# The last MLP of a three-block transformer kernel: the down projection turned, with tokens instead of features on the PSUM partitions

## The chip, the cores and the metric

The kernel runs on one core of one Trainium2 chip. The metric is the device time of one execution in microseconds (us); less is better. The runs of the kernel before gave a median of 1609.58 us.

## The reference, cut to what matters

A chain of three blocks works on 256 latent tokens of 1024 features (and 256 context tokens in the first two). The change lies in the last step of the third block alone: the squared-ReLU MLP with its residual, and the final norm.

```python
def rmsnorm(x, g):
    xf = x.astype(jnp.float32)
    y = xf * lax.rsqrt(jnp.mean(xf * xf, axis=-1, keepdims=True) + NORM_EPS)
    return (y * g.astype(jnp.float32)).astype(x.dtype)
...
D_FF_2 = 4 * D_MODEL          # 4096
...
# last step of the block: h = rmsnorm(x, norm_mlp_g); a = relu(h @ w_up) ** 2; x = x + a @ w_down
# result: rmsnorm(x, norm_final_g)
```

The last two lines are a summary in the kernel's terms. Everything is float32, and the kernel keeps that accuracy by splitting each operand into a high and a low part.

## The kernel before, in words

Activations lie with features on the 128 partitions: `x` is a tile of 8 feature tiles by 512 tokens, and `xs[k]` (128 features by 256 tokens) are the latent tokens' columns. Every float32 product is made of three fp32r products on TensorE, hi x hi, lo x hi and hi x lo (`mm3`, which calls `mm`, L365). A weight chunk is 128 partitions by 1024 numbers, 512 KB. It is loaded on SP's queue into one of 4 buffers `raw` (L349), then `split` makes its high part on ScalarE (`whi`, L343) and its low part on VectorE (`wlo`, L344). `whi` and `wlo` have 3 buffers each, so the split of a chunk waits until TensorE has let go of the chunk three before it. Engines take their instructions in the order that the program's scheduler wrote down; the order cannot change at run time.

The last MLP is the end of `second` (from L1562). Its steps:

- Four chunks `w_ocb` finish the cross attention's output projection (`out2`). Each adds two feature tiles to `x` (L1617).
- `prep` (L520, L521) makes the pair `hm` from `x` times the norm's gains. `sumcols` squares `x` (L552, ScalarE) and sums the squares over the features with a matmul against ones into the bank `ps_nr`; after a small matmul against a constant, `rsqrt` (L398 to L409, nine short VectorE steps) and `bcast` give the row `bcs` of every token's factor, which the first activation needs.
- Up: 32 chunks `w_u`, each one output tile of 128 features by 256 tokens, 8 x 3 = 24 matmuls with the weights stationary and 256 token columns streaming, into one of 4 banks `ps_mm`. The evacuation `ev` is a chain over three engines: VectorE `r` (L1579), GpSimd `a` (L1580), ScalarE `ach` (L343), VectorE `acl` (L344).
- Down: four groups of 8 chunks `w_d`. A chunk of group g holds the weights of one output tile for 8 of the 32 tiles of the activation: again 24 matmuls with stationary weights and 256 streaming columns, into one of two banks `ps_dn`. After each chunk VectorE adds the bank to `x` (L1549). In the last group ScalarE also makes `out`, `x` times the final gains (L1597).
- `AHEAD = 1`: before the down chunks of group g the up chunks run to one beyond the 8 that the group needs.
- Final norm (`rstd_bc`, run as soon as it can be): the squares of seven feature tiles are made between the last down chunks and summed over the features by matmuls against ones (L365, `ps_nr<-sq,ones`); the eighth tile's squares, the root, a broadcast over the partitions by TensorE and eight multiplications follow the last down product (L1601, L1603). Four DMAs of 256 KB write the result.

Of the kernel before, what the change touches and what calls it, by code (L numbers as in the profile page):

```python
# [10 lines left out]
F32 = mybir.dt.float32  # L11
# [8 lines left out]
P = 128  # L20
# [5 lines left out]
# phases in which a product's lo x hi pass comes before its hi x lo pass  # L26
SWAP = ()
# convolutions that take the token after before the token before
TAPS = ('bcw{}', 'fcw0_{}')
# phases that take (y * w) * y in the root's last step, not (y * y) * w  # L30
ROOT = ('pre', 'gmlp', 'gdn', 'ffn0', 'mla', 'ffn1', 'sparse')
MARK = lambda name: None
def weave(*gens):
    """runs the generators step by step in turn."""
    gens = list(gens)
    while gens:
        for g in list(gens):
            if next(g, 0) == 0:
                gens.remove(g)
# [20 lines left out]
# ---------------------------------------------------------------- host layout  # L60
def _fm(w, rows=None):
    """[K, n*128] -> [n, 128, (K/128)*128]: chunk n holds output tile n for every k tile."""
    k, n = w.shape
    return w.reshape(k // P, P, n // P, P).transpose(2, 1, 0, 3).reshape(n // P, P, k)


def _fmx(w, cols):
    """[K, cols] with cols <= 128 -> [1, 128, (K/128)*cols]."""
# [4 lines left out]
def _tm(w, kk):  # L73
    """[K, n*512] -> [n * K/(128*kk), 128, kk*512]."""
# [5 lines left out]
def _cols(v):  # L80
    """[n*128] -> [128, n]."""
# [14 lines left out]
def _consts():  # L96
# [15 lines left out]
    # rows of the (k_idx 64, k_rope 32, w_idx 8) tile spread over 128 partitions  # L112
# [10 lines left out]
    # rope tables, features on partitions  # L123
# [32 lines left out]
def _layout(x):  # L156
    """Lays the inputs out for the chip: name -> array."""
# [4 lines left out]
    x0 = np.concatenate([x["ctx"][0].T, x["x"][0].T], 1)  # [1024, 512]  # L162
# [25 lines left out]
    vec["nfin"] = _cols(x["norm_final_g_2"])  # L188
# [19 lines left out]
    # halves of the input features, two output tiles a chunk  # L208
# [20 lines left out]
    uk = x["w_uk_2"][0]  # [8, 64, 128]  # L229
# [5 lines left out]
    # halves of the input features, two output tiles a chunk  # L235
# [10 lines left out]
    o["w_d2"] = np.stack([_fm(dn[a * 1024:(a + 1) * 1024]) for a in range(4)], 0).reshape(32, P, 1024)  # L246
# [14 lines left out]
# ---------------------------------------------------------------- chip  # L261
class K:
# [25 lines left out]
    def psum(self, **tags):  # L288
        """opens the PSUM banks of a phase: tag -> banks; those of the phase before are closed."""
# [9 lines left out]
    def outer(self, **tags):  # L299
        """closes all PSUM pools; the banks given here outlive the phases that follow."""  # L300
# [18 lines left out]
    def nr(self):  # L319
        """the bank that the norms use."""  # L320
# [20 lines left out]
    # ---- basics  # L341
# [25 lines left out]
    def mm3(self, out, a, b, start, stop):  # L367
        """out += a^T b with a, b as (hi, lo) pairs."""
# [6 lines left out]
    def behind(self, *ins):  # L375
        """what is emitted inside takes its engines' turns after the instructions ins."""
# [13 lines left out]
    def rsqrt(self, v, n, scale=1.0, eps=EPS, plus=None):  # L390
        """(v * scale + eps) ** -0.5 for a [128, n] tile: a guess from the bits, a Newton and a cubic step.
        plus: a tile with eps * RSQ already in it that takes the place of eps."""
# [27 lines left out]
    def rstd_bc1(self, pool, tiles, T):  # L420
        """[128, T] with (mean of the squares over the features in tiles + eps) ** -0.5 of every token."""
# [27 lines left out]
        if n * (T // H) <= 4 and T > H:  # L449
            # groups of 32 rows: one per tile and half  # L450
# [23 lines left out]
    def rstd0(self, pool, tiles):  # L474
        """rstd_bc for 512 tokens, the squares on two engines."""
# [22 lines left out]
    def norm1(self, pool, tiles, T, A, B, hi, lo, halves, bc=None):  # L498
        """hi, lo = split(x * rstd * A + B), A and B per feature (and per half)."""
# [16 lines left out]
    def prep(self, tiles, g, hi, lo):  # L516
        """hi, lo = split(x * g), g per feature; the products' columns get the token's factor later."""
# [5 lines left out]
    def prepb(self, pool, tiles, A, B, hi, lo, soon=True):  # L523
        """hi, lo = split([x * A | B | B]): products with them, their columns times the row returned, plus column
        256, are those with the normalised x * A + B."""
# [16 lines left out]
    def sumcols(self, tiles, T, col=None, tag="nr", pool=None):  # L542
        """[128, T / 128] in PSUM: the sum over all features of (x * col)^2 of every token."""
# [1370 lines left out]
```

## Time and profile before

| what | value |
|---|---|
| median of the runs | 1609.58 us (1602.55, 1609.58, 1613.06) |
| profiled execution, span from first to last instruction | 1609.9 us |
| TensorE busy, share of the span | 97% |
| VectorE, ScalarE, GpSimd busy | 71%, 48%, 13% |
| moved by DMA | 246.27 MB, 153 GB/s |

For the profiled execution the trace gives the span only; no time around it is listed, and the span lies 0.3 us above the median of the runs. Busy time of TensorE counts every matmul from its start to its modelled end, and neighbours overlap, so a fully busy TensorE can still be made faster by issuing fewer columns or fewer matmuls. Starts are exact to 0.01 us, so the spacing of two starts is what a matmul costs.

### The profile page before, as it was taken

The page shows a single profiled execution, that of the slowest core. Times are in us where ns is not written, and L with a number is a line of the kernel's source. Part 1 is how long each engine was busy: PE and PEld are TensorE (multiplying, and loading weights), DVE is VectorE, ACT ScalarE, POOL GpSimd, SP SyncE. Part 2 cuts the span into 40 slices and gives each one's busy share as a digit, 9 for nine tenths or more (in the row PEclk, how much of TensorE's full clock was granted, in tenths as well). Part 3 has the DMA queues.
Part 4 walks back from the last instruction along what each step waited for, and adds up shares of the span by engine and source line. Part 5 has one row for each costly group of instructions (what it writes and reads, how often), then busy time and mean ns, then how long its engine had stood idle before and what let it go on. Part 6 is the DMA issues. An engine that isn't in the chain of part 4 may idle for free.

```text
span 1609.9 us, 28341 instructions
## 1 busy us (share of the span) xinstructions
PE 1553.9 (97%) x10912; PEld 1345.7 (84%) x10912; DVE 1149.8 (71%) x2440; ACT 780.4 (48%) x1422; POOL 202.7 (13%) x191
## 2 busy tenths in 40 slices
PE   7999889999999999999999999999999999999997
PEld 4767667888888888888877799998898898899996
DVE  4556863667999894875676688987897666666663
ACT  4377743445332332353554565656455555444443
POOL 0412100100120120100000021212332000011100
PEclk9999995999999999999999999999999999999999
DMA  8356531343557674633123456565444254345552
GB/s 342 115 201 186 166 105 55 101 139 128 171 183 219 217 234 141 204 118 131 50 63 97 130 173 187 171 193 193 153 127 152 66 176 152 105 157 184 184 183 67
DMA packets 97127, 246.27 MB, mean 153 GB/s; under 512 B 25312, under 2 KB 38368, under 8 KB 96480
## 3 DMA queue, kind: packets, MB, share of 16 engines
q1 hardware_dynamic: 96704, 243.93, 46.9%
q8 instruction: 86, 1.41, 0.4%
q10 hardware_dynamic: 288, 0.52, 0.1%
q14 instruction: 49, 0.40, 0.1%
HBM read 236.30 MB, written 8.13 MB: 152 GB/s over the span
## 4 chain that ended last, share of the span: by engine, by line
PE 88%; DVE 5%; DMA 3%; ACT 2%; issue 1%; SPq 0%; DVEq 0%; ACTq 0%
PE ps_mm L365 52%; PE ps_dn L365 17%; PE ps_nr L365 5%; PE ps_s L365 4%; PE ps_su L365 3%; PE ps_po L365 2%; PE ps_lv L365 1%; DVE wlo L344 1%; DMA rawa<-in_ada 1%; PE ps_ad L365 1%; PE ps_pt L388 1%; ACT whi L343 1%; DMA kvl<-kvd 1%; PE ps_kv L365 1%; PE ps_sm L365 1%
## 5 line engine op out<-in xcount | busy, mean ns | idle before, releaser
L343 ACT ACTIVATE whi<-raw 128x1024 fp32r<-128x1024 f32 (+2 forms) x345 | 346.5, 1008 | 417.5 <-PE ps_mm L365 203.5
L344 DVE TENSOR_TENSOR wlo<-raw,whi 128x1024 fp32r<-128x1024 f32 (+2 forms) x334 | 399.9, 1200 | 128.1 <-ACT whi L343 126.1
L365 PE MATMUL ps_mm<-fh,whi 128*128 128x258 f32 (+2 forms) x728 | 241.6, 333 | 2.6 <-ACT fh L512 1.6
L365 PE MATMUL ps_mm<-fh,wlo 128*128 128x258 f32 (+2 forms) x728 | 241.3, 332 | 0.0
L365 PE MATMUL ps_mm<-fl,whi 128*128 128x258 f32 (+2 forms) x728 | 241.2, 332 | 0.0
L365 PEld LDWEIGHTS ps_mm<-fh,whi 128*128 128x128 f32 x728 | 138.2, 190 | 15.8 <-ACT fh L512 1.8
L365 PEld LDWEIGHTS ps_mm<-fl,whi 128*128 128x128 f32 x728 | 138.3, 190 | 12.7
L365 PEld LDWEIGHTS ps_mm<-fh,wlo 128*128 128x128 f32 x728 | 137.9, 190 | 13.2 <-issue 0.4
L812 POOL TENSOR_TENSOR act<-cg,cu 128x512 f32<-128x512 f32 (+1 forms) x44 | 76.3, 1734 | 465.0 <-DVE cu L750 314.5
L365 PE MATMUL ps_dn<-ah,whi 128*128 128x256 f32 (+1 forms) x366 | 115.8, 319 | 1.6 <-ACT whi L343 1.2
L365 PE MATMUL ps_dn<-ah,wlo 128*128 128x256 f32 (+1 forms) x366 | 115.5, 317 | 0.1
L365 PE MATMUL ps_dn<-al,whi 128*128 128x256 f32 (+1 forms) x366 | 115.1, 316 | 0.0
L675 DVE CUSTOM_DVE_ANT_0 junk<-rawa,cb,vec 128x1024 f32<-128x1024 f32 x80 | 112.7, 1408 | 0.6
L365 PEld LDWEIGHTS ps_dn<-ah,whi 128*128 128x128 f32 x366 | 68.7, 189 | 9.0 <-ACT whi L343 2.4
L365 PE MATMUL ps_mm<-hmh,whi 128*128 128x256 f32 x256 | 72.3, 284 | 2.0 <-DVE r L1579 2.0
L365 PEld LDWEIGHTS ps_dn<-ah,wlo 128*128 128x128 f32 x366 | 68.9, 189 | 6.0 <-DVE wlo L344 0.5
L365 PEld LDWEIGHTS ps_dn<-al,whi 128*128 128x128 f32 x366 | 68.9, 189 | 4.7
L365 PE MATMUL ps_dn<-acl,whi 128*128 128x256 f32 x256 | 72.6, 284 | 0.0
L365 PE MATMUL ps_dn<-ach,whi 128*128 128x256 f32 x256 | 72.3, 284 | 0.3 <-DVE x L1549 0.3
L365 PE MATMUL ps_mm<-hml,whi 128*128 128x256 f32 x256 | 72.5, 284 | 0.0
L365 PE MATMUL ps_dn<-ach,wlo 128*128 128x256 f32 x256 | 72.5, 284 | 0.0
L365 PE MATMUL ps_mm<-hmh,wlo 128*128 128x256 f32 x256 | 72.5, 284 | 0.0
(641 smaller groups left out, 4014.7 us busy)
## 6 DMA issues: line engine op xcount, KB each, us to landing
raw<-in_up SPq DMA_DIRECT2D x88, 512.0 KB, 3.5
rawa<-in_adt SPq DMA_DIRECT2D x56, 512.0 KB, 4.0
rawa<-in_ada SPq DMA_DIRECT2D x40, 512.0 KB, 7.2
raw<-in_dn SPq DMA_DIRECT2D x40, 448.0 KB, 3.4
raw<-in_w_u SPq DMA_DIRECT2D x32, 512.0 KB, 4.2
raw<-in_w_d SPq DMA_DIRECT2D x32, 512.0 KB, 4.0
raw<-in_w_qkvg SPq DMA_DIRECT2D x16, 512.0 KB, 3.8
raw<-in_dn SPq DMA_DIRECT2D x16, 512.0 KB, 3.5
```

What stands on the lines that cost most here:

```text
L343: self.nc.scalar.activation(hi, src, AF.Copy)
L344: (eng or self.nc.vector).tensor_tensor(lo, src, hi.bitcast(F32), op=ALU.subtract)
L365: self.nc.tensor.matmul(out, lhsT, rhs, start=start, stop=stop, **kw)
L388: self.nc.tensor.transpose(out, in_, self.ident[:in_.shape[0], :in_.shape[0]])
L675: self.nc.vector.tensor_tensor_reduce(o, r, self.cb[:, c], 1.0, self.v(f"ada_b{l}", i), ALU.mult, ALU.add, m[:, i, c:c + 1])
L812: nc.gpsimd.tensor_tensor(a, cg, cu, op=ALU.mult)
```

## The change

The down projection is turned. A `w_d` chunk now holds the weights of two activation tiles for 512 output features; the activation (128 features by 128 tokens) is stationary and the weights stream 512 columns. The four sums (two token tiles by two halves of the features) stay in four PSUM banks over all 32 activation tiles, in 16 groups of two up chunks and two down chunks; the up products have three banks. Of the down projection's 768 matmuls of 256 columns 384 matmuls of 512 columns become. The 32 additions to `x` go. For the residual, `x` is transposed at the start of the MLP by 16 small TensorE transposes into `xt`, tokens on partitions (four ScalarE copies). At the end each bank is added to `xt`, ScalarE squares the sum and sums it along the row, so the final norm needs no matmul; its gains come as one row on all partitions (`gf`, one more DMA of 512 KB on SP's queue, ahead of the first `w_u`). The result is written as rows of tokens. Comments that the diff also takes out are not shown.

```diff
-    vec["nfin"] = _cols(x["norm_final_g_2"])
...
-    o["w_d2"] = np.stack([_fm(dn[a * 1024:(a + 1) * 1024]) for a in range(4)], 0).reshape(32, P, 1024)
+    o["w_d2"] = dn.reshape(16, 2, P, 2, 512).transpose(0, 3, 2, 1, 4).reshape(32, P, 1024)
+    o["nfin"] = x["norm_final_g_2"].reshape(1, 1024)
...
-            out = pool.tile([P, 8, 256], F32, name="outt", tag="outt", bufs=1)
+            xt = pool.tile([P, 2, 1024], F32, name="xt", tag="xt", bufs=1)
+            gf = pool.tile([P, 1024], F32, name="gf", tag="gf", bufs=1)
+            nc.sync.dma_start(gf, d["nfin"][0].partition_broadcast(P))
+            for t in range(2):
+                for n in range(2):
+                    ps = self.ps("dn")
+                    for k in range(4):
+                        self.tr(ps[:, k * P:(k + 1) * P], xs[4 * n + k][:, t * P:(t + 1) * P])
+                    nc.scalar.activation(xt[:, t, n * 512:n * 512 + 512], ps, AF.Copy)
             acts = []
...
-            for g in range(4):
-                n = min(32, 8 * g + 8 + AHEAD)
+            self.psum(mm=3, dn=4)
+            acc = {(t, n): self.ps("dn") for t in range(2) for n in range(2)}
+            for g in range(16):
+                n = min(32, 2 * g + 2 + AHEAD)
                 self.gemm([d["w_u2"][j] for j in range(len(acts), n)], 8, P, hi, lo, 256, ev)
-                for j in range(8):
-                    wh, wl = self.chunk(d["w_d2"][g * 8 + j])
-                    wh = wh.rearrange("p (k m) -> p k m", k=8)
-                    wl = wl.rearrange("p (k m) -> p k m", k=8)
-                    ps = self.ps("dn")
-                    for k in range(8):
-                        self.mm3(ps[:, :256], (wh[:, k], wl[:, k]), acts[8 * g + k], k == 0, k == 7)
-                    self.add_x(j, ps[:, :256])
-                    if g == 3:
-                        nc.scalar.activation(out[:, j], xs[j], AF.Copy, scale=self.v("nfin", j))
-            bc = self.rstd_bc(pool, xs, 256)
-            for k in (6, 0, 7, 1, 2, 3, 4, 5):
-                if k >= 6:
-                    nc.gpsimd.tensor_tensor(out[:, k], out[:, k], bc[1], op=ALU.mult)
-                else:
-                    nc.vector.tensor_tensor(out[:, k], bc[0], out[:, k], op=ALU.mult)
-            for k in (0, 2, 4, 6):
-                (nc.sync, nc.scalar)[k // 2 % 2].dma_start(d["out"][:, k:k + 2], out[:, k:k + 2])
+                ws = [[w.rearrange("p (k m) -> p k m", k=2) for w in self.chunk(d["w_d2"][2 * g + n])] for n in range(2)]
+                turns = [(t, n) for n in range(2) for t in range(2)] if g < 15 else list(acc)
+                for t, n in turns:
+                    wh, wl = ws[n]
+                    for q in range(2):
+                        k = 2 * g + q
+                        s = slice(t * P, (t + 1) * P)
+                        ah, al = acts[k][0][:, s], acts[k][1][:, s]
+                        self.mm(acc[t, n], ah, wh[:, q], k == 0, False)
+                        self.mm(acc[t, n], ah, wl[:, q], False, False)
+                        self.mm(acc[t, n], al, wh[:, q], False, k == 31)
+            for t in range(2):
+                ss = self.t(pool, [P, 2], "ss", 2)
+                for n in range(2):
+                    o = xt[:, t, n * 512:n * 512 + 512]
+                    nc.vector.tensor_tensor(o, acc[t, n], o, op=ALU.add)
+                    nc.scalar.activation(self.t(pool, [P, 512], "sq", 2), o, AF.Square, accum_out=ss[:, n:n + 1])
+                og = self.t(pool, [P, 512], "og", 2)
+                nc.gpsimd.tensor_tensor(og, xt[:, t, 512:], gf[:, 512:], op=ALU.mult)
+                v = self.t(pool, [P, 1], "vs", 2)
+                nc.vector.tensor_tensor(v, ss[:, 0:1], ss[:, 1:2], op=ALU.add)
+                r = self.rsqrt(v, 1, 1.0 / 1024)
+                for n in range(2):
+                    o = xt[:, t, n * 512:n * 512 + 512]
+                    if n:
+                        o = og
+                        nc.scalar.activation(o, o, AF.Copy, scale=r)
+                    else:
+                        nc.vector.scalar_tensor_tensor(o, o, r, gf[:, :512], op0=ALU.mult, op1=ALU.mult)
+                    (nc.sync, nc.scalar)[n].dma_start(d["out"][t * P:(t + 1) * P, n * 512:n * 512 + 512], o)
```

On every engine the order of the instructions is the same in both kernels up to the end of the `w_ocb` chunks (SP's queue up to the `gf` load). Three places after that matter.

TensorE at the start of the MLP. In the order of before, the first up chunk (`ps_mm_15893`) follows the last `w_ocb` product (`ps_mm_15791`) at once, and the squares' sums (`ps_nr`) are spread between its products:

```order
L365 MATMUL ps_mm_15791<-och_15317,wlo_15788 128x256
L365 MATMUL ps_mm_15893<-hmh_15683,whi_15889 128x256
L365 MATMUL ps_mm_15893<-hml_15684,whi_15889 128x256
L365 MATMUL ps_mm_15893<-hmh_15683,wlo_15890 128x256
...
L365 MATMUL ps_mm_15893<-hmh_15683,whi_15889 128x256
L365 MATMUL ps_nr_15834<-sq_15847,ones 32x256
L365 MATMUL ps_mm_15893<-hml_15684,whi_15889 128x256
```

In the order of the changed kernel the 16 transposes (from `x` into `ps_dn`) and the rest of the sums stand there, and the first up chunk (`ps_mm_15927`) comes behind them:

```order
L366 MATMUL ps_mm_15791<-och_15317,wlo_15788 128x256
L389 MATMUL ps_dn_15889<-c_61,x 128x128 x4
L389 MATMUL ps_dn_15895<-c_61,x 128x128 x2
L366 MATMUL ps_nr_15834<-sq_15847,ones 32x256
L366 MATMUL ps_nr_15834<-sq_15850,ones 32x256
L389 MATMUL ps_dn_15895<-c_61,x 128x128 x2
L389 MATMUL ps_dn_15901<-c_61,x 128x128 x4
L366 MATMUL ps_nr_15834<-sq_15853,ones 32x256
L366 MATMUL ps_nr_15834<-sq_15856,ones 32x256
L389 MATMUL ps_dn_15907<-c_61,x 128x128 x4
L366 MATMUL ps_nr_15834<-c_61,ssb_15859 128x1 x2
L366 MATMUL ps_mm_15927<-hmh_15683,whi_15923 128x256
```

What moved: nothing covers the waits of these small matmuls for ScalarE and VectorE any more, since no up product stands between them.

TensorE in a group of the middle. Before, a down chunk runs behind an up chunk (`ps_mm_16205`) through the activation's tiles into one bank:

```order
L365 MATMUL ps_mm_16205<-hmh_15683,wlo_16202 128x256
L365 MATMUL ps_dn_16244<-ach_15922,whi_16240 128x256
L365 MATMUL ps_dn_16244<-acl_15923,whi_16240 128x256
L365 MATMUL ps_dn_16244<-ach_15922,wlo_16241 128x256
L365 MATMUL ps_dn_16244<-ach_15961,whi_16240 128x256
```

Now, behind the second up chunk of a group (`ps_mm_16233`), the products go over four banks (15917 to 15920) with two weight chunks (`whi_16268`, `whi_16274`); `ach_16148` is the activation that the group before left over, `ach_16223` that of the up chunk just before `ps_mm_16233`:

```order
L366 MATMUL ps_mm_16233<-hmh_15683,wlo_16230 128x256
L366 MATMUL ps_dn_15917<-wlo_16269,ach_16148 128x512
L366 MATMUL ps_dn_15917<-whi_16268,acl_16149 128x512
L366 MATMUL ps_dn_15919<-wlo_16269,ach_16148 128x512
L366 MATMUL ps_dn_15919<-whi_16268,acl_16149 128x512
L366 MATMUL ps_dn_15918<-whi_16274,ach_16148 128x512
L366 MATMUL ps_dn_15920<-whi_16274,ach_16148 128x512
L366 MATMUL ps_dn_15917<-whi_16268,ach_16223 128x512
L366 MATMUL ps_dn_15917<-wlo_16269,ach_16223 128x512
```

What moved: both chunks of a group are held until close to its end, and an activation is used 24 + 6 matmuls after the up chunk that made it, not up to 200 matmuls later.

VectorE at the end. Before:

```order
L1549 TENSOR_TENSOR x<-ps_dn_18140,x 128x256
L446 TENSOR_SCALAR plus_18167<-ps_nr_18168 128x2
L400 SCALAR_TENSOR_TENSOR rq_18200<-ps_nr_18195,plus_18167 128x2
...
L409 SCALAR_TENSOR_TENSOR rq_18208<-rq_18207,rq_18204 128x2
L1603 TENSOR_TENSOR outt<-ps_nr_18218,outt 128x256 x6
```

Now there are four additions (`xt`) and two roots, one per token tile:

```order
L1616 TENSOR_TENSOR xt<-ps_dn_15917,xt 128x512
L1616 TENSOR_TENSOR xt<-ps_dn_15918,xt 128x512
L1616 TENSOR_TENSOR xt<-ps_dn_15919,xt 128x512
L1616 TENSOR_TENSOR xt<-ps_dn_15920,xt 128x512
L1621 TENSOR_TENSOR vs_17754<-ss_17745 128x1
...
L1621 TENSOR_TENSOR vs_17787<-ss_17778 128x1
L405 SCALAR_TENSOR_TENSOR rq_17759<-rq_17758,rq_17756 128x1
...
L1629 SCALAR_TENSOR_TENSOR xt<-xt,rq_17764,gf 128x512
...
L1629 SCALAR_TENSOR_TENSOR xt<-xt,rq_17797,gf 128x512
```

What moved: no matmul stands in this chain any more, and in the middle of the first root VectorE waits for the second tile's sum of squares.

## Rows read from the trace of the kernel before

**Rows 1.** The page: busy time of the engines, and TensorE's granted clock in 40 slices.

```profile
PE 1553.9 (97%) x10912; PEld 1345.7 (84%) x10912; DVE 1149.8 (71%) x2440; ACT 780.4 (48%) x1422; POOL 202.7 (13%) x191
...
PEclk9999995999999999999999999999999999999999
```

**Rows 2.** Windows: stretch, its length, busy us (instructions) per engine, PEclk, DMA share, GB/s.

```profile
1402.59:1598.10 195.51, 193.25 (x1566) 187.21 (x1564) 118.80 (x169) 85.99 (x114) 19.99 (x32) 1.00 0.49 158
...
1440.00:1480.00 40.00, 40.00 (x336) 40.00 (x334) 25.20 (x35) 17.77 (x21) 4.31 (x7) 1.00 0.56 183
```

**Rows 3.** Windows of the splits of raw chunks alone: DVE, ACT, POOL busy (splits).

```profile
1429.08:1570.20 141.12, 61.99 (x49) 51.92 (x50) 0.00 (x0) 1.00 0.56 183
```

**Rows 4.** Timeline of TensorE: start, us, matmul; 512 columns, weights stationary, then activations stationary.

```profile
440.05 0.39 PE L365 MATMUL ps_mm<-fh,wlo 128*128 128x512 f32 x1
...
451.61 0.39 PE L365 MATMUL ps_mm<-fh,wlo 128*128 128x512 f32 x1
...
1208.22 0.39 PE L365 MATMUL ps_mm<-wlo,hh 128*128 128x512 f32 x1
...
1209.15 0.39 PE L365 MATMUL ps_mm<-whi,hl 128*128 128x512 f32 x1
```

**Rows 5.** Timeline of TensorE: a square's sum of the final norm between down products.

```profile
1594.48 0.28 PE L365 MATMUL ps_dn<-ach,whi 128*128 128x256 f32 x1
1594.69 0.62 PE L365 MATMUL ps_nr<-sq,ones 128*32 128x256 f32 x2
...
1595.46 0.28 PE L365 MATMUL ps_dn<-ach,wlo 128*128 128x256 f32 x1
```

**Rows 6.** Timeline of TensorE: the end of the fourth up chunk, the wait, the fifth.

```profile
1417.36 0.28 PE L365 MATMUL ps_mm<-hmh,wlo 128*128 128x256 f32 x1
...
1420.26 0.39 PE L365 MATMUL ps_mm<-hmh,whi 128*128 128x256 f32 x1 [1.98 <-DVE r L1579]
```

**Rows 7.** Timeline of TensorE: four float32 transposes (two records each) and the matmul behind them.

```profile
118.94 1.04 PE L388 MATMUL ps_s<-c,w 128*128 128x128 f32 x8
119.74 0.48 PE L365 MATMUL ps_mm<-h0lo,whi 128*128 128x512 f32 x1
```

**Rows 8.** Timelines of VectorE, GpSimd and ScalarE: one up chunk's evacuation, a chunk's split.

```profile
1432.08 0.42 DVE L1579 SCALAR_TENSOR_TENSOR r<-ps_mm,bcs 128x256 f32<-128x256 f32 x1 [0.28 <-PE ps_mm L365]
...
1432.65 0.61 POOL L1580 TENSOR_TENSOR a<-r 128x256 f32<-128x256 f32 x1 [2.26 <-DVE r L1579]
...
1433.29 0.42 ACT L343 ACTIVATE ach<-a 128x256 fp32r<-128x256 f32 x1 [0.27 <-POOL a L1580]
1434.84 1.06 ACT L343 ACTIVATE whi<-raw 128x1024 fp32r<-128x1024 f32 x1 [1.13 <-PE ps_mm L365]
...
1435.93 1.29 DVE L344 TENSOR_TENSOR wlo<-raw,whi 128x1024 fp32r<-128x1024 f32 x1 [0.55 <-ACT whi L343]
```

**Rows 9.** The chain that ended last, in order of time: start, us, what.

```profile
1575.84 0.44 DVE x L1549
...
1598.26 0.56 PE ps_nr L365 x2
...
1604.68 1.32 DVE outt L1603 x4
```

**Rows 10.** Groups by form: count, busy us, mean ns of one, idle before; one row of a timeline.

```profile
L1617 DVE TENSOR_TENSOR x<-ps_mm,x 128x512 f32<-128x512 f32 x12 | 8.3, 690 | 9.3 <-PE ps_mm L365 9.3
L507 DVE SCALAR_TENSOR_TENSOR nt<-cz,vec,ps_nr 128x512 f32<-128x512 f32 x1 | 0.7, 746 | 0.2 <-ACT rbc L471 0.2
...
L485 ACT ACTIVATE sq<-x 128x512 f32<-128x512 f32 x4 | 2.3, 622 | 3.3 <-DMA x<-in_x 1.8 <-PE ps_sm L365 1.5
...
1372.20 0.20 ACT L1417 ACTIVATION_READ_ACCUMULATOR p<-ps_s,mx,rc 128x1 f32 x1
```

**Rows 11.** The last use of the cross attention's values (count, ns, first and last start); SP's queue.

```profile
L365 PE MATMUL ps_po<-pph,vcl x16: 276/280/284, 1366.8 to 1381.1; 128*128 128x256 f32 x16
...
1382.91 31.66 SPq L349 DMA_DIRECT2D raw<-in_w_u  x9
```

More of the change, by code (lines that the diff above doesn't have):

```diff
@@ L1907 @@
         d[name] = nc.dram_tensor(f"in_{name}", a.shape, F32, kind="ExternalInput").ap()
-    d["out"] = nc.dram_tensor("out_0", (P, 8, 256), F32, kind="ExternalOutput").ap()
+    d["out"] = nc.dram_tensor("out_0", (256, 1024), F32, kind="ExternalOutput").ap()
     with tile.TileContext(nc, schedule_with_timeline_sim=True) as tc:
@@ L1912 @@
     got = r.results[0]["out_0"]
-    return np.ascontiguousarray(got.transpose(2, 1, 0).reshape(1, 256, 1024))
+    return np.ascontiguousarray(got.reshape(1, 256, 1024))
```

## The prediction

> **What bounds the kernel now.** I read the page first: TensorE is busy for 97% of the span, and its granted clock is 0.9 or more of full speed in 39 of 40 slices [rows 1]. The two orders agree up to the end of the `w_ocb` chunks, so the change can only move time behind 1402.59 us, where the last MLP's first product starts. The windows of that stretch come next [rows 2]: 195.5 us to the end of the down products, TensorE busy for 193.3 of them at clock 1.00, VectorE for 118.8, ScalarE for 86.0. In 1440 to 1480 us TensorE and its weight loads fill all 40 us. The splits confirm it: a split waits until TensorE lets go of a buffer, and 49 of them start in 141.12 us, one in 2.88 us [rows 3]. A chunk is 24 matmuls, so a 256-column matmul costs 2.88 / 24 = 0.1200 us, up and down alike, with no wait between groups. So the number and length of TensorE's instructions set this stage; VectorE's 32 additions cost nothing here, except the one that TensorE waits for in the last group.
>
> TensorE's 195.5 us are 1536 x 0.120 = 184.3 us of products and 11.2 us of other things: ten squares' sums that stand between products (four of the MLP's norm, six of the final norm), two small sums (0.2), that one wait (0.5), and a wait of 3 us before the fifth up chunk. A square's sum costs 0.74: from 1594.48 to 1595.46 there are two product steps and one sum, 0.98 - 0.24 [rows 5]. So 10 x 0.74 = 7.4, and 7.4 + 0.2 + 0.5 + 2.8 = 10.9 accounts for all but 0.3.
>
> **The change part by part.**
>
> Down products: 768 x 0.120 us become 384 matmuls of 512 columns. With weights stationary, 51 steps from 440.05 to 451.61 give 0.2267; with activations stationary and weights streaming, as the change has it, four steps from 1208.22 to 1209.15 give 0.2325 [rows 4]. I take 0.2267, because that stretch too is one where TensorE is fed without a break: 384 x (0.2400 - 0.2267) = -5.1 us. The other end is 384 x (0.2400 - 0.2325) = -2.9. The columns are the same number; what is saved is a fixed part of each matmul, 2 x 0.1200 - 0.2267 = 0.0133 us.
>
> The trace puts that fixed part at 13 ns for each of the 384 matmuls that vanish [rows 3, 4]. The Trainium skill ("TensorE: Matmul & The Clock Gate", section "Back-to-back issue gap") gives 262 cycles for 256 columns and 518 for 512, so two halves cost only 6 cycles more than a whole; by that this term would be an estimated 1.0 us, not 5.1, and the total about 4 us later. The trace's rows are of this kernel's own mix of weight loads and matmuls, and I go by them.
>
> Final norm: the six sums between the down products go, 6 x 0.74 = -4.4 us, and with the additions to `x` goes the wait of 0.5 us at 1575.84 [rows 9]. ScalarE's squares move behind the last product.
>
> Start: 16 float32 transposes come in. Four take 119.74 - 118.94 = 0.80 us with the change of operand behind them [rows 7], so 16 x 0.2 = +3.2. The four sums and the small matmuls stay, but now stand together ahead of the first up chunk. They wait for the last pair of feature tiles: addition, ScalarE's gains and squares, the sum, one more copy. By the same order I reckon 6.3 us from the last `w_ocb` product to the first up product, of which 3.2 + 4 x 0.74 + 0.2 = 6.4 are work already, so hardly a wait; if ScalarE, which has four copies of 0.6 us more in its queue there, is late at each, up to 2 us. In return the factors `bcs` come earlier against the up products: VectorE makes the root straight after the sum, with no splits between, and only three up chunks run before the first down chunk. The wait of 1420.26 - 1417.36 - 0.12 = 2.8 us [rows 6] shrinks to the broadcast's two matmuls, 0.4. Start: 3.2 - 2.4 = +0.8 (from -0.5, where the sums get cheaper side by side, to +2.8).
>
> `gf` is one more DMA ahead of `w_u` on SP's queue. It waits for memory that the cross attention read until 1381.1; the first `w_u` was issued at 1382.91 [rows 11], for a split that came some 10 us later. I cost it at nothing; without that cover the first up chunk would be later by some 4 us.
>
> Groups of the middle: 16 waits could appear, because only three split buffers exist and a group holds two of them. I follow one group, its first up product at 0. The up chunks end at 2.9 and (with two down products between) 6.2, the down products at 11.2; so 16 x 11.2 replaces 64 x 2.88. The weights: the buffer of the first down chunk falls free at the 18th of the 22 last products, 10.4; the next group's second up chunk is split by 11.6 (`whi`, 1.06 [rows 8]) and 12.9 (`wlo`), and needed at 14.1 and 14.8. The next first down chunk has its `whi` at 12.7, needed at 14.3: 1.6 us to spare, the tightest place. The activation: `r` starts 0.4 after the chunk's end, and `ach` ends 1.6 later (1432.08 to 1433.71 [rows 8]), at 4.9; it is needed at 7.5. So 0 us, with 1.6 us of slack a group.
>
> End: before, 11.8 us lie between 1598.10 and the span's end. Now the four additions start while the last three products run (0.69 each [rows 10]), and ScalarE's four squares (0.62 + 0.20 for the row's sum) end 3.7 us after the last product's start. VectorE, stopped in the first root for the second tile's sum, goes on at 3.8: the short steps of two roots, 0.2 each, 15 of them, and two multiplications of 0.75 (the row with two factors) end at 8.4. Before, the last multiplication ended at 1606.0 [rows 9] and the span 3.9 later with the result's DMA; with the same 3.9 the end is 12.3 after the last product's start, against 11.9 before: +0.4 (-1 to +2).
>
> Sum: -5.1 - 4.4 - 0.5 + 0.8 + 0.4 = -8.8 us. On the profiled execution 1609.9 - 8.8 = 1601.1; the median of the runs is 0.3 below its span, so **1600.8 us**, 0.55% less. A measurement of this kernel can tell about 1% from no change, so I expect "the same".
>
> **The rivals.**
>
> *The gain is half of that.* The turned products keep the 0.2325 us that the only turned stretch shows, and ScalarE is late at the start and the end: -2.9 - 4.4 - 0.5 + 2.8 + 2.0 = -3.0, about 1606.5. For it: that stretch is the nearest in form. Against it: it lies in a stage where other things interrupt TensorE. A fixed part of a matmul that is smaller than the rows show would end in the same span: at a quarter of 0.0133 us the first term is -1.3 and the sum -5.0, 1604.6. That is the case of the section named above.
>
> *The split buffers starve TensorE (slower).* Place: `whi` of the group's first down chunk, behind `whi` of the up chunk on ScalarE's queue, both behind the release near the group's end; behind it there wait the second down chunk's split and `ach`. It decides from 1.6 us of delay on; 0.55 us of wait a group would undo the whole gain. If splits could not overlap the turned products at all, a group would wait for a `whi` and a `wlo`, 1.06 + 1.29 = 2.35 us [rows 8]: 16 x 2.35 - 8.8 = +28.8, 1638. Against it: the margins above, and a chunk's split ran inside 2.88 us 49 times running [rows 3].
>
> *The clock falls.* One slice of the 40 was granted half speed [rows 1], so it can happen in this program. At 1.2 instead of 2.4 GHz a turned product would cost at most another 0.2267 us; if a third of the 384 ran so, +29 - 8.8, about 1630. Against it: in the stretch of the turned products at 1208 us the slice shows 0.9 or more, and nothing idles here. The Trainium skill (same page, section "A second HAM failure mode: psum-queue depth-cycling") says that cycling through PSUM banks at 512 columns can make TensorE idle briefly and its clock swing; the trace does not bear it out for this kernel.
>
> *More than forecast*: the sums side by side and a shorter end give -12, 1598; beyond that only the spread of the runs (1602.55 to 1613.06) helps.
>
> **How the numbers follow.** Forecast (1598 to 1604) 0.55, half gain 0.27, starved 0.08, clock 0.03, more 0.07. The forecast and the half gain span 1598 to 1607; with the runs' own spread of about 5 us to either side, a bit less below, the range is 1594 to 1612, which leaves out the starved and the clock cases. Faster by over 1% (below 1593.5) needs the spread on top of the best case: 0.07. Slower by over 1% (above 1625.7) is most of the starved and the clock cases: 0.07. The rest, 0.86, is within 1%.
>
> **What would show it.** Right: in the middle of the MLP 512-column products 0.227 us apart, a group in 11.2 us, weight loads of TensorE less busy, no wait on `whi` or `ach`; some 6.4 us between the last `w_ocb` product and the first up product; no `ps_nr` behind the broadcast; the last down product near 1588.9; 12.3 us from there to the end. Wrong: groups longer than 11.5 us with TensorE waiting for `whi`, `wlo` or `ach`; a granted clock below 0.9 behind 1420 us; steps of 0.2325 or more; an end longer than 14 us.

## The result and the profile after

The changed kernel took 1601.55 us in the median of 20 runs (1580.31 to 1604.94), the kernel before 1613.6 us on the same chip (20 runs): ratio 0.9919, 95% interval 0.9895 to 0.9943, so 0.8% less. The ratio is that of the fast runs; the two medians, which take in all runs, would give 0.9925. The profiled execution has a span of 1600.1 us against 1609.9.

First the page of the changed kernel, to hold against [rows 1]:

```profile
PE 1543.2 (96%) x10518; PEld 1325.5 (83%) x10518; DVE 1137.7 (71%) x2418; ACT 778.1 (49%) x1418; POOL 203.8 (13%) x191
...
PEclk9999985899999999999999999999999999999998
```

TensorE is busy 10.7 us less, and of its clock the seventh slice shows half speed, as before, with 0.8 on either side of it and in the last slice, where the end stands and TensorE has almost nothing to do. The windows of the last MLP, from the end of the `w_ocb` products to the end of the down products, and of 40 us in its middle (columns as in [rows 2]):

```profile
1404.15:1588.88 184.73, 184.57 (x1186) 166.81 (x1184) 104.23 (x139) 81.43 (x104) 19.63 (x32) 1.00 0.54 168
1440.00:1480.00 40.00, 40.00 (x252) 36.22 (x251) 21.86 (x29) 17.48 (x22) 4.29 (x7) 1.00 0.63 192
```

184.73 us stand where 195.51 stood [rows 2], at the same granted clock. TensorE is still the engine without a gap, but its weight loads now fill 36.2 of 40 us in place of all 40.

The stage began 1.56 us later in this execution (1404.03 against 1402.47 us for the start of the last `w_ocb` product), although the two programs agree up to there; in the profiles of this study that start lies anywhere from 1398.84 to 1405.11 us. That part of the program is where the whole times scatter, so from here on I compare two lengths that do not hold it: the *stage*, from the start of the last `w_ocb` product to the start of the last down product, and the *end*, from there to the end of the span.

| profile | stage, us | end, us | both | against the changed kernel |
|---|---|---|---|---|
| before | 195.51 | 11.92 | 207.43 | +11.36 |
| changed | 184.62 | 11.45 | 196.07 | |
| changed, profiled again (e10_after_again) | 184.63 | 11.49 | 196.12 | +0.05 |
| e1_split256 | 189.62 | 10.65 | 200.27 | +4.20 |
| e2_one_square (of before) | 191.09 | 11.30 | 202.39 | -5.04 against before |
| e3_no_turn | 184.85 | 11.51 | 196.36 | +0.29 |
| e4_turn_late | 186.13 | 11.51 | 197.64 | +1.57 |
| e5_ahead2 | 184.70 | 10.50 | 195.20 | -0.87 |
| e6_no_pool | 184.63 | 11.01 | 195.64 | -0.43 |
| e7_one_root | 184.70 | 10.09 | 194.79 | -1.28 |
| e8_in_banks | 187.03 | 9.34 | 196.37 | +0.30 |
| e9_vector_og | 184.70 | 9.66 | 194.36 | -1.71 |

The two profiles of the changed kernel agree within 0.05 us, so I take these lengths to tell tenths apart where the whole times cannot; every other row is one profiled execution.

The place where the stage starts, on TensorE (start, us, matmul, records):

```profile
1404.03 0.28 PE L366 MATMUL ps_mm<-och,wlo 128*128 128x256 f32 x1
1404.15 0.82 PE L389 MATMUL ps_dn<-c,x 128*128 128x128 f32 x6
1404.89 0.63 PE L366 MATMUL ps_nr<-sq,ones 128*32 128x256 f32 x4
1405.45 1.03 PE L389 MATMUL ps_dn<-c,x 128*128 128x128 f32 x6
1406.52 1.33 PE L366 MATMUL ps_nr<-sq,ones 128*32 128x256 f32 x4
1407.78 0.66 PE L389 MATMUL ps_dn<-c,x 128*128 128x128 f32 x4
1408.47 0.61 PE L366 MATMUL ps_nr<-c,ssb 128*128 128x1 f32 x4
1408.93 0.36 PE L366 MATMUL ps_mm<-hmh,whi 128*128 128x256 f32 x1
```

The sixteen transposes are sixteen records here. Six of them take 1404.89 - 1404.15 = 0.74 us, 0.12 each; two sums of squares side by side take 1405.45 - 1404.89 = 0.56, 0.28 each, where one between products cost 0.74 [rows 5]. The second pair of sums waits for ScalarE, whose queue in the same stretch reads:

```profile
1404.22 1.06 ACT L344 ACTIVATE whi<-raw 128x1024 fp32r<-128x1024 f32 x1 [1.77 <-PE ps_mm L366]
...
1406.77 0.40 ACT L553 ACTIVATE sq<-x 128x256 f32<-128x256 f32 x1
1407.08 1.06 ACT L1583 ACTIVATE xt<-ps_dn 128x512 f32<-128x512 f32 x2
1408.03 0.38 ACT L559 ACTIVATE ssb<-ps_nr 128x256 f32<-128x256 f32 x1
```

So 4.90 us lie between the last `w_ocb` product and the first up product. Behind it TensorE meets one more interruption, the two matmuls that broadcast the norm's factors (`rq` into `ps_nr`, from which `bcs` is made):

```profile
1413.33 0.28 PE L366 MATMUL ps_mm<-hmh,whi 128*128 128x256 f32 x1
1413.45 0.60 PE L366 MATMUL ps_nr<-c,rq 128*128 128x128 f32 x4
1413.81 0.36 PE L366 MATMUL ps_mm<-hml,whi 128*128 128x256 f32 x1
```

They take 1413.81 - 1413.33 - 0.12 = 0.36 us, and no wait for `bcs` comes behind them, where 2.8 us stood before [rows 6]. In the middle, twelve steps of the turned products:

```profile
1585.03 0.39 PE L366 MATMUL ps_dn<-whi,acl 128*128 128x512 f32 x1
...
1587.75 0.39 PE L366 MATMUL ps_dn<-wlo,ach 128*128 128x512 f32 x1
```

2.72 / 12 = 0.2267 us, the value of [rows 4]. A group (48 up products, 24 down products) lasts from the first of these rows to the second, 11.22 us:

```profile
1440.96 0.40 PE L366 MATMUL ps_dn<-wlo,ach 128*128 128x512 f32 x1
...
1452.18 0.40 PE L366 MATMUL ps_dn<-wlo,ach 128*128 128x512 f32 x1
```

And the end, all engines:

```profile
1587.97 1.07 PE L366 MATMUL ps_dn<-whi,acl 128*128 128x512 f32 x4
1588.40 2.48 DVE L1616 TENSOR_TENSOR xt<-ps_dn,xt 128x512 f32<-128x512 f32 x4 [2.70 <-PE ps_dn L366]
...
1589.77 2.50 POOL L1619 TENSOR_TENSOR og<-xt,gf 128x512 f32<-128x512 f32 x2 [4.97 <-DVE xt L1616]
...
1590.80 0.26 DVE L1621 TENSOR_TENSOR vs<-ss 128x1 f32<-128x1 f32 x1
...
1591.47 0.81 DVE L404 TENSOR_TENSOR rq<-rq 128x1 f32<-128x1 f32 x1
1591.53 0.19 ACT L1617 ACTIVATION_READ_ACCUMULATOR sq<-xt 128x1 f32 x1
...
1595.75 0.72 ACT L1627 ACTIVATE og<-og,rq 128x512 f32<-128x512 f32 x1 [1.49 <-DVE rq L410]
```

The last down product starts at 1587.97 + 3 x 0.227 = 1588.65. All four banks close within the last four products, four additions follow in a row, and two roots, one behind the other, on VectorE. (`vs` adds the two sums of squares of a token tile, the `rq` are the steps of a root, `og` is the second 512 columns times the final gains.) One square of a single column takes 0.81 us; it ends at 1592.28, and GpSimd's second product ends at 1592.27.

### The profile page after: what moved, and what is told of

Its sections match the earlier page's. It is cut to its first block, busy times and chain, and to the rows that moved or that the text cites. A ratio compares the mean times of both kernels' runs of the same rounds, so it can differ in the third digit from the quotient of the medians.

```text
span 1600.1 us, 27482 instructions
## 1 busy us (share of the span) xinstructions
PE 1543.2 (96%) x10518; PEld 1325.5 (83%) x10518; DVE 1137.7 (71%) x2418; ACT 778.1 (49%) x1418; POOL 203.8 (13%) x191
## 4 chain that ended last, share of the span: by engine, by line
PE 87%; DVE 5%; DMA 4%; ACT 3%; issue 1%; SPq 1%; ACTq 0%; DVEq 0%
PE ps_mm L366 51%; PE ps_dn L366 17%; PE ps_nr L366 4%; PE ps_s L366 4%; PE ps_su L366 3%; PE ps_po L366 2%; PE ps_lv L366 1%; DVE wlo L345 1%; DMA rawa<-in_ada 1%; PE ps_pt L389 1%; ACT whi L344 1%; PE ps_ad L366 1%; DMA kvl<-kvd 1%; PE ps_kv L366 1%; DMA raw<-in_w_qkvg 1%
## 5 line engine op out<-in xcount | busy, mean ns | idle before, releaser
L366 PEld LDWEIGHTS ps_mm<-fh,wlo 128*128 128x128 f32 x728 | 137.4, 189 | 13.3 <-issue 0.4
L366 PE MATMUL ps_mm<-hh,whi 128*128 128x256 f32 (+1 forms) x224 | 65.7, 295 | 2.1 <-DVE z L1717 1.7
L366 PE MATMUL ps_mm<-hl,whi 128*128 128x256 f32 (+1 forms) x224 | 64.2, 288 | 0.0
L366 PE MATMUL ps_mm<-hh,wlo 128*128 128x256 f32 (+1 forms) x224 | 63.8, 286 | 0.0
```

Source lines behind the costliest of these rows:

```text
L366: self.nc.tensor.matmul(out, lhsT, rhs, start=start, stop=stop, **kw)
```

## The experiments

**e1_split256: narrow products in the turned form.** Theory: what the down products win is the fixed part of a matmul. Rival: it is the room on VectorE.

```diff
-self.mm(acc[t, n], ah, wh[:, q], k == 0, False)
-self.mm(acc[t, n], ah, wl[:, q], False, False)
-self.mm(acc[t, n], al, wh[:, q], False, k == 31)
+for c in (slice(0, 256), slice(256, 512)):
+    self.mm(acc[t, n][:, c], ah, wh[:, q, c], k == 0 and c.start == 0, False)
+    self.mm(acc[t, n][:, c], ah, wl[:, q, c], False, False)
+    self.mm(acc[t, n][:, c], al, wh[:, q, c], False, k == 31 and c.start > 0)
```

> Every 512-column down product is made as two of 256 columns into the same bank; the same weights, activations, banks, final norm and order otherwise, so VectorE is spared as much as in the change. Theory (the gain of the down products is the fixed part of a product, 2 x 0.1200 against 0.2267 us, 384 times): a group of three loads lasts 11.52 us in place of 11.215, the stage from the last w_ocb product to the last down product is 5.1 us longer than in the changed kernel, the whole near 1606.5 us on its median (ratio to before 0.995). Rival (the gain comes from the 32 additions that VectorE no longer makes and the room that this gives the splits): the group stays at 11.2 and the time at that of the change, within 1 us.

Measured: ratio to before 0.9961 (0.9941 to 0.9982), median 1606.33 us. The windows of the stage and of its middle:

```profile
1405.15:1594.77 189.62, 189.45 (x1570) 187.29 (x1568) 106.44 (x141) 83.52 (x105) 19.59 (x32) 1.00 0.49 163
1440.00:1480.00 40.00, 40.00 (x336) 40.00 (x335) 23.33 (x29) 17.53 (x22) 4.90 (x8) 1.00 0.55 184
```

The stage is 189.62 - 184.62 = 5.00 us longer, with VectorE busy for the same share (56%) as in the changed kernel. 5.00 / 384 = 13.0 ns for each matmul more: the theory's 13.3. The weight loads fill all 40 us again, as before. Each matmul more also brings a weight load more (1568 against 1184), so the 13 ns are the price of the pair; no run here parts the two. VectorE has the room and the 5 us are gone all the same, so the rival is out. The end is 0.80 us shorter than the changed kernel's, because the additions start 1.11 us ahead of the last product's start (1593.54 and 1594.65), in place of 0.25.

**e2_one_square: the kernel before without six sums between its products.**

```diff
-bc = self.rstd_bc(pool, xs, 256)
+bc = self.rstd_bc(pool, xs[7:], 256)
```

> The kernel before, its final norm's sum of squares taken over the last feature tile alone (seven tiles' squares and six of the sums between products are left out, so it is not the norm any more). Theory (each of the six sums costs TensorE 0.74 us between products): 4.4 us less before the last down product, and up to 0.8 more behind it, -4.4 to -5.2 us against before, ratio 0.997. Rival (the sums fill places where TensorE would wait for a weight or an eviction): under 0.5 us less before the last product, ratio 0.999 to 1.000.

Measured: ratio 0.9949 (0.9925 to 0.9974). Two rows of TensorE, the last `w_ocb` and the last down product:

```profile
1405.11 0.28 PE L365 MATMUL ps_mm<-och,wlo 128*128 128x256 f32 x1
...
1596.20 0.28 PE L365 MATMUL ps_dn<-ach,wlo 128*128 128x256 f32 x1
```

191.09 us, 4.42 less than before; the end is 0.62 shorter. Six sums at 0.74 are 4.44. The sums were not hidden.

**e3_no_turn: the changed kernel without the transposes.**

```diff
-ps = self.ps("dn")
-for k in range(4):
-    self.tr(ps[:, k * P:(k + 1) * P], xs[4 * n + k][:, t * P:(t + 1) * P])
-nc.scalar.activation(xt[:, t, n * 512:n * 512 + 512], ps, AF.Copy)
+nc.gpsimd.memset(xt[:, t, n * 512:n * 512 + 512], 0.0)
```

> The changed kernel without the sixteen transposes of x: the tile that should hold x with tokens on partitions is set to zero by GpSimd, so the residual is left out. Theory as forecast (sixteen transposes take 3.2 us of TensorE's time ahead of the first products up): 4.95 us between the last w_ocb product and the first product up fall to about 2 to 3, and the two sums of squares go back to between the products. Rival (they stand where TensorE waits for ScalarE and VectorE, as before's 2.8 us wait there, and four evictions of theirs lengthen ScalarE's chain): the time falls by 0 to 1.5 us against the changed kernel.

Measured: ratio 0.9927 (0.99 to 0.9953). The first up product starts 0.76 us behind the last `w_ocb` product, but the stage is 0.23 us *longer*. TensorE then meets its own chain:

```profile
1410.44 0.62 PE L366 MATMUL ps_nr<-sq,ones 128*32 128x256 f32 x2
1413.84 0.50 PE L366 MATMUL ps_nr<-c,ssb 128*128 128x1 f32 x4
1417.28 0.68 PE L366 MATMUL ps_nr<-c,rq 128*128 128x128 f32 x4 [0.68 <-DVE rq L410]
1419.22 0.39 PE L366 MATMUL ps_mm<-hmh,whi 128*128 128x256 f32 x1 [1.26 <-DVE r L1586]
```

The last sum stands between products again, `ssb` 3.4 us behind it, and the up products wait for banks whose eviction needs `bcs`. So with no transposes at all nothing is won: where the change puts them they stand in time that TensorE would wait anyway. What they cost with the sums left where the changed kernel has them is not shown, because the order of the sums changed with them.

**e4_turn_late: the transposes behind the third up chunk.** The block of transposes goes from ahead of `acts` to behind this line, with nothing else changed:

```diff
+self.gemm([d["w_u2"][j] for j in range(3)], 8, P, hi, lo, 256, ev)
```

> The changed kernel with the sixteen transposes of x behind the third up chunk in place of ahead of the first; nothing else. Measured as the time from the last w_ocb product to a late up product, less 0.12 us for each product between (before: 6.37 us, the changed kernel: 5.42, without transposes: 5.63). Theory (the start is bounded by the chain through ScalarE and the root to the tile bcs, and the transposes only fill TensorE's wait for it): 5.2 to 5.9 us, the whole within 0.6 us of the changed kernel apart from where the last stage begins. Rival (sixteen transposes cost TensorE their 2.5 us wherever they stand): near 8 us.

Measured in a single execution: 6.92 us beside products, between the two forecasts; the stage is 1.51 us longer than the changed kernel's.

```profile
1416.07 1.04 PE L389 MATMUL ps_dn<-c,x 128*128 128x128 f32 x8
1417.74 1.15 PE L389 MATMUL ps_dn<-c,x 128*128 128x128 f32 x8 [0.64 <-ACT xt L1594]
```

They fill part of the wait for `bcs`, but with two banks the second eight wait for ScalarE's copies of the first. Against 5.63 us without transposes that is a cost of 1.3. So neither theory holds as written: the place decides, and of the two places tried the change's is the better one.

**e5_ahead2: the products up two chunks ahead.**

```diff
-AHEAD = 1
+AHEAD = 2
```

> The changed kernel with the products up two chunks ahead of those down in place of one, so the last up product stands a group earlier and the last group need not end with the four products that wait for the last activation's low part. Theory (the end of 11.5 us is VectorE's four additions in a row and two roots one behind the other, because all four banks close within 0.9 us): the banks close 1.36 us apart, three additions and the first root begin before the last product ends, and from the last product to the end 8.5 to 9.5 us pass in place of 11.5; the time is 2 to 3 us below the changed kernel. Rival (the end is set by the second token tile's chain of addition, square, root, product and transfer whatever the first does): under 0.5 us less. The stage before it stays at 11.2 us a group in both.

Measured: ratio 0.9918 (0.9897 to 0.9939); the end is 10.50 us, 0.95 less, a third to a half of what the theory said and more than the rival.

```profile
1589.40 0.39 PE L366 MATMUL ps_dn<-whi,acl 128*128 128x512 f32 x1
...
1589.83 0.69 DVE L1616 TENSOR_TENSOR xt<-ps_dn,xt 128x512 f32<-128x512 f32 x1 [0.44 <-PE ps_dn L366]
...
1591.17 0.81 DVE L404 TENSOR_TENSOR rq<-rq 128x1 f32<-128x1 f32 x1
```

The banks close apart and three additions are over before the last product ends, as expected. But the first root still begins behind the fourth addition in VectorE's order, stalls for 0.81 us in its third step, and from the end of that step (1591.98) to the end of the span 7.9 us pass, as in the changed kernel (1592.28 to 1600.1, 7.8).

**e6_no_pool: without GpSimd's two products at the end.**

```diff
-nc.gpsimd.tensor_tensor(og, xt[:, t, 512:], gf[:, 512:], op=ALU.mult)
...
-    o = og
-    nc.scalar.activation(o, o, AF.Copy, scale=r)
+    nc.scalar.activation(og, o, AF.Copy, scale=r)
+    o = og
```

> The changed kernel without GpSimd's two products of the second 512 columns with the final norm's weight (that weight is left out of half of the output); ScalarE scales xt into og instead. Theory (VectorE's small two-input operations wait while GpSimd works: the root's first square took 0.81 us and ended when GpSimd's second product ended, against 0.16 elsewhere): that square takes 0.16 us, the sum vs 0.15 in place of 0.26, and the end from the last down product to the end is 0.5 to 0.7 us shorter. Rival (that square waits for the second token tile's sum of squares, which lands at about the same moment): the root pauses for as long at the next instruction, the end is as long as before within 0.15 us.

Measured in a single execution: the end 11.01 us, 0.44 less, between the theory's 0.5 to 0.7 and the rival's 0.15.

```profile
1588.80 0.16 DVE L404 TENSOR_TENSOR rq<-rq 128x1 f32<-128x1 f32 x1
...
1589.19 0.16 DVE L1620 TENSOR_TENSOR vs<-ss 128x1 f32<-128x1 f32 x1 [0.23 <-ACT sq L1617]
```

The square takes 0.16 us, so its 0.81 was GpSimd's doing. Of the 0.65 us saved there a third comes back: the next step in the queue is the second token tile's `vs`, and it now waits 0.23 us for ScalarE, as the rival had it.

**e7_one_root: one root for both token tiles, on top of e5.**

```diff
-v = self.t(pool, [P, 1], "vs", 2)
-nc.vector.tensor_tensor(v, ss[:, 0:1], ss[:, 1:2], op=ALU.add)
-r = self.rsqrt(v, 1, 1.0 / 1024)
+nc.vector.tensor_scalar(pl, ss[0], RSQ / 1024, EPS * RSQ, op0=ALU.mult, op1=ALU.add)
...
+r = self.rsqrt(ss[1], 2, 1.0 / 1024, plus=pl)
```

> The changed kernel with products up two chunks ahead, and one root over both token tiles (128 x 2) in place of two roots one behind the other; the sum of the first half's squares goes into the root's first step by a step made ahead. Theory (the end is VectorE's two roots in a row): nine short steps of 0.195 us and one sum fewer, the first scaled row half a microsecond later and the last one 1.2 to 1.6 us earlier, from the last down product to the end 9.0 to 9.4 us in place of 10.5 with two roots; time 1 to 1.5 us below the run with two chunks ahead, 2 to 2.5 below the changed kernel. Rival (the output transfers, started at two times before and now together, take up what is won): under 0.5 us.

Measured: ratio 0.9928 (0.9875 to 0.9981); the end 10.09 us, 0.41 less than e5 and longer than the theory's 9.0 to 9.4.

```profile
1589.27 2.50 POOL L1620 TENSOR_TENSOR og<-xt,gf 128x512 f32<-128x512 f32 x2 [9.36 <-DVE xt L1617]
...
1591.17 0.61 DVE L401 SCALAR_TENSOR_TENSOR rq<-ss,vs 128x2 f32<-128x2 f32 x1 [0.85 <-ACT sq L1618]
...
1593.39 1.42 DVE L1627 SCALAR_TENSOR_TENSOR xt<-xt,rq,gf 128x512 f32<-128x512 f32 x2
...
1594.20 0.98 ACTq L1630 DMA_DIRECT2D out<-og  x2
```

The last scaled row is done at 1594.81 (e5: 1596.17, so 1.4 us earlier in the profile's time and 1.2 against the last product). Now the root's first step is the one that GpSimd holds up, and from the last row to the end 4.5 us pass in place of 3.7: four transfers issued within a microsecond land later than two and two. In e8 and e9, which issue them together too, it is 4.4 and 4.3; why they take longer is not shown. Both theory and rival had a part.

**e8_in_banks: x turned by products with the identity into the four banks, on top of e7.**

```diff
-self.tr(ps[:, k * P:(k + 1) * P], xs[4 * n + k][:, t * P:(t + 1) * P])
...
+self.mm(acc[t, n][:, k * P:(k + 1) * P], xs[4 * n + k][:, t * P:(t + 1) * P], self.ident, k == 0, False)
```

> As the run with one root, and x is turned by products with the identity straight into the four accumulation banks, in place of transposes, copies to SBUF and additions at the end; the squares, the product with the weight (on VectorE, none on GpSimd) and the scaling read the banks. Theory (the last bank's addition of 0.69 us stands between the last product and its square): 0.7 to 1.2 us less at the end than with one root alone, 3 to 3.5 us below the changed kernel; the start the same within 0.5 us, since what TensorE does there fills a wait. Rival (a product with the identity takes more of TensorE's time than a transpose and the squares from the banks are slower): the gain at the end is given back at the start, within 0.5 us of the run with one root.

Measured: ratio 0.9931 (0.9906 to 0.9955); the end 9.34 us, 0.75 less than e7, but the stage 2.33 us longer. Most of the 0.75 is not the theory's doing: this run also takes GpSimd's products away, and e9 below, which does only that, has 0.43 of it. Reading the banks brings the other 0.32.

```profile
1405.09 3.17 PE L366 MATMUL ps_dn<-c,x 128*128 128x128 f32 x26
...
1420.62 0.39 PE L366 MATMUL ps_mm<-hmh,whi 128*128 128x256 f32 x1 [0.70 <-DVE r L1589]
```

Each float32 product with the identity is two records of 0.12 us where a transpose is one, and the sums of squares are again late. The rival was right in kind, and the loss at the start is three times the gain at the end.

**e9_vector_og: e7 with the weight's products on VectorE.**

```diff
-nc.gpsimd.tensor_tensor(og[t], o, gf[:, 512:], op=ALU.mult)
+nc.vector.tensor_tensor(og[t], o, gf[:, 512:], op=ALU.mult)
```

> As the run with one root, the two products with the final norm's weight for the second 512 columns on VectorE in place of GpSimd. Theory (in the run with one root the first step of the root took 0.61 us and ended with GpSimd's second product): that step takes 0.16 us; the two products of about 0.65 us on VectorE lie while the last squares are summed, but the last bank's addition comes 0.2 us later; from the last down product to the end 9.6 to 9.9 us in place of 10.1, the time 0.3 to 0.5 us below the run with one root and 1.5 to 2 us below the changed kernel. Rival (VectorE's queue is what is full there): no gain, 10.0 to 10.3 us.

Measured: the end 9.66 us, within the theory's 9.6 to 9.9.

```profile
1583.54 0.39 PE L366 MATMUL ps_dn<-whi,acl 128*128 128x512 f32 x1
...
1585.70 0.16 DVE L401 SCALAR_TENSOR_TENSOR rq<-ss,vs 128x2 f32<-128x2 f32 x1
```

**e10_after_again: the changed kernel once more, beside e9.**

> The changed kernel as it is, on the same chip as the run before it, so that the two are compared with each other: ratio to before 0.990 to 0.995; 4.9 us from the last w_ocb product to the first product up, a group in 11.2 us, 11.45 us from the last down product to the end as in its first profile.

Measured: 184.63 and 11.49 us, first up product 4.91 us behind the last `w_ocb` product; ratio 0.9939 (0.9921 to 0.9958). e9 on the same chip: median 1599.93 against 1601.78 us, ratio to before 0.9947 (0.9915 to 0.9979). By the two lengths e9 is 1.7 us faster than the changed kernel and 13.1 than the kernel before; the whole times, which scatter by 5 us and more, do not tell e9 from the changed kernel.

## Why the prediction was right, point by point

The forecast time (1600.8 us) lies 0.75 from the measured median, and that closeness is luck: the median fell by 12.05 us where 8.8 were forecast, and the median that the forecast started from (1609.58, of three runs) lay 4.02 below that of all twenty. The interval of the ratio is within 1% of no change but for its lower edge (0.9895), as expected. The sum is the better test: -8.8 us forecast, -11.36 measured over stage and end (-10.89 and -0.47). The forecast place of the last down product, near 1588.9, came out at 1588.65 by luck too, because the stage began 1.56 us later in that execution; the stage itself is 1.7 us shorter than forecast.

- *Down products*: -5.1 forecast; e1 shows 5.00. The spacing of 0.2267 us was right, 0.2325 was not. By the cycle counts of the Trainium skill ("TensorE: Matmul & The Clock Gate", section "Back-to-back issue gap") this term would be an estimated 1.0 us; the section gives them for isolated matmuls and says that in a stream the weight loads set the spacing too. For this stream of weight loads and matmuls the runs decide: 5.00.
- *Six sums*: -4.4; e2 shows 4.42.
- *The wait for the additions to x*: -0.5. Not tried alone; 10.89 - 5.00 - 4.42 - 0.95 (the start, below) leaves 0.52 for it.
- *Start*: +0.8 forecast, -0.95 measured (5.42 us in place of before's 6.37, counted as in e4's expectation: from the last `w_ocb` product to a late up product, less 0.12 for each product between), below the stated lower edge of -0.5. This is the term that was mis-sized. Of its two parts the -2.4 held: the wait of 2.8 us for `bcs` shrank to the broadcast's 0.36, where 0.4 was forecast. The +3.2 for the transposes came out as about +1.5. The step "four take 0.80 us, so 16 x 0.2 = +3.2" read eight transposes as four: in the changed kernel sixteen transposes are sixteen records, so the eight records of [rows 7] are eight transposes of 0.10 each, and 0.12 is what each of six side by side took. And the four sums were priced at 0.74 where they stand side by side at 0.28; the text gave that as the lower edge only. The last `w_ocb` product with 0.12, the transposes with 16 x 0.12, the sums with 4 x 0.28 and the two small sums with 0.46 (1408.47 to 1408.93) are 3.6 us of work in the 4.90 us ahead of the first up product, where 6.3 to 6.4 were forecast. The other 1.3 are waits for ScalarE, "hardly a wait" in the forecast's value and "up to 2 us" in its bound. e3 shows that with no transposes at all nothing is won.
- *Groups of the middle*: no wait forecast, none measured (TensorE is busy for all of the 40 us in the middle); 11.2 us forecast, 11.22 measured. `gf` cost nothing that can be seen.
- *End*: 12.3 us forecast, 11.45 measured; against before +0.4 forecast and -0.47 measured, within the stated -1 to +2 but of the other sign. The order of steps was right, each a little cheaper: squares over at 3.1 us in place of 3.7, the multiplications at 7.8 in place of 8.4, the transfer 3.7 in place of 3.9. What the prediction laid to the second tile's sum, VectorE stopped in the first root, was mostly GpSimd (e6).

The rivals: *half the gain* asked for steps of 0.2325 us and a start 2.8 us longer; the steps were 0.2267 and the start shorter. *Starved split buffers* asked for waits on `whi` or `wlo`; TensorE had none. *The clock* stayed at 1.00 in the stage. The last slice's 0.8 lies below the 0.9 that the prediction named as a sign of this case, but it belongs to the end, where TensorE has next to nothing left to do: the mean granted clock is 0.63 from 1589.00 to 1600.10 us, between the levels of 2.4 and 1.2 GHz, as it is 0.73 at the end of before, from 1598.10 to 1609.90. *More than forecast* (-12, "the sums side by side and a shorter end") is what came in the stage and the end, with -11.4; it had a chance of 0.07 and deserved more, since the cheaper sums and a shorter end were both named as possible; the start then fell below even its stated lower edge.

## What to carry to other kernels

Where TensorE runs without a gap, count matmuls and their neighbours: the same columns in half as many matmuls saved 13 ns for each one gone, and a small product of another shape cost 0.74 us between large ones and 0.28 beside its like. Put layout work such as transposes where TensorE waits for a chain on other engines; there leaving sixteen of them out won nothing, while a few microseconds later they cost 1.3 us. And before a duration is divided by a count, find out how many records one instruction leaves.

## What the runs showed of the hardware that was not expected

A VectorE operation with two inputs in SBUF, of one or two columns only, waits until a GpSimd product ends: 0.81 us (ending at 1592.28, GpSimd at 1592.27), 0.81 in e5 (1591.98, 1591.96), 0.61 in e7 (1591.78, 1591.77), and 0.16 without GpSimd (e6, e9). `vs` at 1590.80 fits as well: it ended at 1591.06, when the first of GpSimd's two products, 1.25 us each, was over (1591.02). The root's steps with a single input just ahead of the 0.81 (at 1591.09 and 1591.28) took their 0.15 us beside GpSimd, and the additions, with one input in PSUM, kept their 0.62 us spacing. The Trainium skill ("SBUF — State Buffer", section "Who interferes with whom") states this rule: a VectorE instruction with two SBUF inputs contends with a GpSimd instruction that reads SBUF, and the port pair that they share is an exclusive lock. The traces here agree as far as VectorE waiting for GpSimd goes; GpSimd waiting for VectorE is not shown.

Removing work from the busiest engine made a stage longer (e3): TensorE works in the order that the scheduler wrote, and without the transposes that order had the products ahead of the sums that everything else waited for.
